# A decoder block on one core: the norm factor's broadcast moved, q and k turned in other lumps, q, k, v weights at another address, and the second norm's sum taken mid chunk

## Chip, cores and metric

The kernel runs on one core of a Trainium2 chip. The metric is the device time of one execution in microseconds: 377.47 us, the median of three runs (377.06 to 378.2). Lower is better.

## What is computed

One decoder layer over x (1, 256, 1024) in float32, cut to what matters:

```python
h = rms_norm(x, attn_norm_g)
qa, ka, va, qb, kb, vb, f_logit, g_logit = split(h @ w_in)     # six of 512 columns, 8, 2 x 1024
qa, ka = partial_rope(rms_norm(heads(qa))), partial_rope(rms_norm(heads(ka)))
o_a = causal softmax(qa ka^T / 8) va      # MoBA: with 256 tokens there is one block, so plain causal
qb, kb = rms_norm(heads(qb)), rms_norm(heads(kb))
c = cumsum(log_sigmoid(f_logit + b_forget))
o_b = causal softmax(qb kb^T / 8 + c[t] - c[s]) vb             # forgetting attention (FoX)
merged = sigmoid(g0 + b0) * (o_a @ w_branch_moba) + sigmoid(g1 + b1) * (o_b @ w_branch_fox)
x = x + merged @ w_out
u, g = split(rms_norm(x, ffn_norm_g) @ w_ffn_up)               # 2 x 2816 columns
x = x + (silu(causal_conv3(g) + b) * u) @ w_ffn_down
```

Eight heads of 64 in each branch.

## The kernel before

Everything is float32 at nearly full precision: each operand of a large product is split into a high part (fp32r, written by ScalarE, the whi or xh tiles) and the rest (by VectorE, wlo or xl), and each product is three matmuls, hi x hi, hi x lo and lo x hi. The weights come in 61 chunks of 128 x 2048 floats (1 MB), loaded by DMAs on SyncE's queue into one of three raw buffers. `load` splits a chunk in two halves of 1024 columns, each into one of six whi and six wlo tiles. `use(c, h)` hands out a half and has splits issued up to five halves ahead, so that ScalarE and VectorE work ahead of TensorE until the six buffers are full.

x is kept transposed (features on the partitions), as xh and xl times the norm's gain; the norm's factor rs per token is multiplied in after the products. The order of TensorE's instructions is that of the program text, by hand; the order on the other engines is a planner's, with dependencies, so it may change when the text is moved. PSUM has eight banks of 512 floats; all tiles there come from one pool of eight, and `banks()` takes two.

- `project(m, pt, h)`: one half of a q, k or v product (m = 0 to 2 the MoBA branch's q, k, v, 3 to 5 the FoX branch's), tokens on the partitions. 24 matmuls at line 217: 128 columns of xh or xl are loaded into the array and 512 columns of whi or wlo stream.
- `twin(kind, c, dst, mh, ml)`: a chunk of 2 x 128 output features, features on the partitions. 48 matmuls at lines 425 to 427: 128 columns of the weights are loaded and 256 tokens of mh or ml stream. The gates and the FFN's up product use it. Lines 512 to 514, 538 to 540 and 599 to 601 are the same form for the branch, out and down products.
- `norm1` (line 195): the sum of squares over partitions for rs; `rsqrt_mean` (lines 182 to 187) is VectorE, ScalarE's Ln and Exp, and three steps on VectorE.
- `rs_row` (413, 414): four matmuls with the identity broadcast rs to all partitions as rsB, which the gates read at line 432.
- `forget_a` to `forget_d` and `forget_bias`: the forget gate. `forget_a` (279, 283) multiplies by the eight gate columns wfg; `forget_b` (292 to 312) gives lf; `forget_c` (318 to 321) is the cumulative sum; `forget_d` (326 to 332) turns it, writes it to memory and reads it back on all partitions into one of the three raw buffers; `forget_bias` (339, 341) makes the bias from it.
- `finish_qk` (229 to 245): the heads' norms and rope; `turn_qk` (261, 266, 268): 16 transposes of 64 x 64, and copies by ScalarE and VectorE into qT or kT.
- `scores` (355) and `softmax` (367 to 375) for pairs of heads, `turn` (385, 388) turns the probabilities into pT, `values` (399, 403, 404) multiplies by V into oh and ol, `finish_v` (221) writes V.

The text that orders the first stage:

```python
    norm1(); rs_row(); forget_a()
    qn = finish_qk(pq, 0, 0)
    project(1, pk, 1)
    kn = finish_qk(pk, 0, 1)
    project(2, pv, 0); forget_b(); turn_qk(qn, 0, 0)
    project(2, pv, 1); turn_qk(kn, 0, 1); finish_v(pv, 0)
    project(3, pq, 0); forget_c(); scores(0, (0, 1))
    project(3, pq, 1); qn = finish_qk(pq, 1, 0); forget_d(); scores(0, (2, 3))
    project(4, pk, 0); turn(0, 0); turn(0, 1)
    project(4, pk, 1); kn = finish_qk(pk, 1, 1); turn(0, 2); turn(0, 3); turn_qk(qn, 1, 0)
    project(5, pv, 0); forget_bias(); values(0)
    project(5, pv, 1); turn_qk(kn, 1, 1); finish_v(pv, 1); gate(0)
```

The out product (line 540) is followed, for each pair of feature blocks, by the new x (543), its split into hh and hl (546, 547; these lie in the oh and ol buffers), its squares (549), and their running sum sqs on GpSimd (551 to 554). The FFN runs 22 chunks of `up`, two at a time, and after each pair but the first the `down` product of the pair before. In `up(0)` the sum of squares over partitions (565) and rs2 by `rsqrt_mean` follow the chunk's 48 matmuls. Behind them each `up` multiplies by rs2 (568), does the convolution (572 to 574), Silu (575), and splits the result (580, 581) into a tile in qT, kT or aT, which `down` streams.

Addresses: a tile's gaps at the head of the pool place the whi and wlo tiles at 32 mod 256 bytes; behind them a gap of 96 bytes and 16 bytes inside the tile place xh, xl, oh, ol and the later activations. All tiles between are multiples of 256 bytes long.

Of the kernel before, what the change touches and what calls it, by code (L numbers as in the profile page):

```python
# [9 lines left out]
F32R = mybir.dt.float32r  # L10
BF16 = mybir.dt.bfloat16
AF = mybir.ActivationFunctionType
# [5 lines left out]
P = 128  # L18
S = 256
NT = 2  # L20
D = 1024
KT = D // P
# [8 lines left out]
RB, HB, AHEAD = 3, 6, 5  # L31
# [10 lines left out]
def decoder_block(ctx, tc, a, out):  # L42
    nc = tc.nc
# [6 lines left out]
    def T(shape, tag, bufs=1, dt=F32):  # L50
        return sb.tile(shape, dt, tag=tag, bufs=bufs, name=tag)
# [11 lines left out]

    gap("gap0", GAPS[0])
    for tag in ("whi", "wlo"):
        T([P, 1024], tag, HB, F32R)
    gap("gap1", GAPS[1])
    for tag in ("xh", "xl", "oh", "ol"):
        T16(KT, tag)
# [19 lines left out]
    def load(upto):  # L89
        while state["next"] <= min(upto, 2 * len(chunks) - 1):  # L90
            i, h = divmod(state["next"], 2)
            c = chunks[i]
            n = 2 if i < 2 else 1
            if h == 0:
                w = 512 if i < 2 else 1024 if i == 2 else 2048
                src = a[c[0]]
                for j in c[1:]:
                    src = src[j]
                raw = state["raw"] = T([P, 2048], "raw", RB)
                for j in range(2048 // w):  # L100
                    if i < 2:
                        for k in XCUT.get(4 * i + j, ()):
                            load_x(k)
                    nc.sync.dma_start(raw[:, j * w:(j + 1) * w], src[:, j * w:(j + 1) * w])
            raw = state["raw"][:, h * 1024:(h + 1) * 1024]
            hi = T([P, 1024], "whi", HB, F32R)
            lo = T([P, 1024], "wlo", HB, F32R)
            w = 1024 // n
            for j in range(n):
                s = slice(j * w, (j + 1) * w)  # L110
                if i < 2:
                    split_x(2 * (2 * i + h) + j)
                nc.scalar.activation(hi[:, s], raw[:, s], AF.Copy)  # L113
                nc.vector.tensor_tensor(lo[:, s], raw[:, s], hi[:, s].bitcast(F32), op=ALU.subtract)  # L114
            split[c, h] = (hi, lo)
            state["next"] += 1
# [61 lines left out]
    def rsqrt_mean(dst, ss, n, shape, tag, bufs=2):  # L178

        w = T([P, 3] + shape, tag, bufs)  # L180
        v, y, t = w[:, 0], w[:, 1], w[:, 2]
        nc.vector.tensor_scalar(v, ss, 1.0 / n, EPS, op0=ALU.mult, op1=ALU.add)
        nc.scalar.activation(t, v, AF.Ln)
        nc.scalar.activation(y, t, AF.Exp, scale=-0.5)
        nc.vector.scalar_tensor_tensor(t, v, -0.5, y, op0=ALU.mult, op1=ALU.mult)
        nc.vector.tensor_tensor(t, t, y, op=ALU.mult)
        nc.vector.scalar_tensor_tensor(dst, t, 1.5, y, op0=ALU.add, op1=ALU.mult)

    rs = T([P, NT], "rs")
    rope = []  # L190
# [18 lines left out]
    def project(m, pt, h):  # L209
        for hh in range(2):  # L210
            wh, wl = use(("qkv", m, h), hh)
            for k2 in range(2):
                k = 4 * h + 2 * hh + k2
                rh, rl = wh[:, k2 * 512:(k2 + 1) * 512], wl[:, k2 * 512:(k2 + 1) * 512]
                for i, (lhs, rhs) in enumerate(((xh, rh), (xh, rl), (xl, rh))):
                    for t in range(NT):
                        nc.tensor.matmul(pt[t], lhs[:, k, t * P:(t + 1) * P], rhs, start=(k == 0 and i == 0), stop=(k == KT - 1 and i == 2))  # L217
# [70 lines left out]
    def forget_b():  # L288
        fs = fg["fs"]
        ft = bank()  # L290
        for t in range(NT):
            nc.tensor.matmul(ft[:, t * NH:(t + 1) * NH], fs[:, t * P:(t + 1) * P], sel, start=True, stop=True)
        z = T([P, NT, NH], "z")
        for t in range(NT):
            nc.vector.scalar_tensor_tensor(z[:, t], ft[:, t * NH:(t + 1) * NH], rs[:, t:t + 1], col(C_BF, NH), op0=ALU.mult, op1=ALU.add)

        az = T([P, NT, NH], "az")
        nc.scalar.activation(az, z, AF.Abs)
        e = T([P, NT, NH], "ez")
        nc.scalar.activation(e, az, AF.Exp, scale=-1.0)  # L300
        u = T([P, NT, NH], "uz")
        nc.vector.tensor_scalar_add(u, e, 1.0)
        l = T([P, NT, NH], "lz")
        nc.scalar.activation(l, u, AF.Ln)
        d = T([P, NT, NH], "dz")
        nc.vector.scalar_tensor_tensor(d, u, -1.0, e, op0=ALU.add, op1=ALU.subtract)
        r = T([P, NT, NH], "rz")
        nc.vector.reciprocal(r, u)
        nc.vector.tensor_tensor(d, d, r, op=ALU.mult)
        nc.vector.tensor_tensor(l, l, d, op=ALU.subtract)  # L310
        lf = T([P, NT, NH], "lf")
        nc.vector.scalar_tensor_tensor(lf, z, 0.0, l, op0=ALU.min, op1=ALU.subtract)
        fg["lf"] = lf
# [96 lines left out]
    def rs_row():  # L410
        rp = bank()
        for t in range(NT):
            nc.tensor.matmul(rp[:, t * P:(t + 1) * P], rs[:, t:t + 1].to_broadcast([P, P]), ident, start=True, stop=True)
        nc.vector.tensor_copy(rsB, rp[:, 0:S])

    def twin(kind, c, dst, mh, ml):

        for h in range(2):
            wh, wl = use((kind, c), h)
            for i in range(2):  # L420
                o = dst[:, i * S:(i + 1) * S]
                for k4 in range(4):
                    k = 4 * h + k4
                    w = slice(k4 * 256 + i * P, k4 * 256 + (i + 1) * P)
                    nc.tensor.matmul(o, wh[:, w], mh[:, k], start=(k == 0 and i == 0), stop=False)  # L425
                    nc.tensor.matmul(o, wh[:, w], ml[:, k], start=False, stop=False)  # L426
                    nc.tensor.matmul(o, wl[:, w], mh[:, k], start=False, stop=(k == KT - 1 and i == 1))  # L427

    def gate(c):
        gp = bank()  # L430
# [3 lines left out]
    def gate_sigmoid(c):  # L434
        for br in range(2):
            i = nc.scalar.activation(gates[:, c, br], gates[:, c, br], AF.Sigmoid, bias=col(C_BG + br * KT + c))
            after(i, last_exp[0])

    def after(i, j):
        tc.add_manual_dep(i.ins, j.ins.name, mybir.DependencyInfo(mybir.DependencyClass.NoSync, mybir.DependencyReason.DATA), reason="order")  # L440
# [6 lines left out]
    project(0, pq, 1)  # L447
    project(1, pk, 0)
    norm1()
    rs_row()  # L450
    forget_a()
    qn = finish_qk(pq, 0, 0)
    project(1, pk, 1)
    kn = finish_qk(pk, 0, 1)
    project(2, pv, 0)
    forget_b()
    turn_qk(qn, 0, 0)
    project(2, pv, 1)
    turn_qk(kn, 0, 1)
    finish_v(pv, 0)  # L460
    pq, pk, pv = banks(), banks(), banks()
    project(3, pq, 0)
    forget_c()
    scores(0, (0, 1))
    project(3, pq, 1)
    qn = finish_qk(pq, 1, 0)
    forget_d()
    scores(0, (2, 3))
    project(4, pk, 0)
    turn(0, 0)  # L470
    turn(0, 1)
    project(4, pk, 1)
    kn = finish_qk(pk, 1, 1)
    turn(0, 2)
    turn(0, 3)
    turn_qk(qn, 1, 0)
    project(5, pv, 0)
    forget_bias()
    values(0)
    project(5, pv, 1)  # L480
    turn_qk(kn, 1, 1)
    finish_v(pv, 1)
    gate(0)
# [11 lines left out]
    values(1)  # L495
    gate(6)
    gate(7)
    for c in range(KT):
        gate_sigmoid(c)


    mh = T16(KT, "xh")
# [57 lines left out]

    def up(f):
        up_ = bank()
        twin("wu", f, up_, hh, hl)
        if f == 0:
            nc.tensor.matmul(sp[:, 0:S], ones, sqs, start=True, stop=True)
            rsqrt_mean(rs2, sp[:, 0:S], D, [S], "pT", 4)
        ev = T([P, 2, S], "sq", 2)
        nc.vector.tensor_tensor(ev, up_.rearrange("p (b t) -> p b t", b=2), rs2[:, None, :].to_broadcast([P, 2, S]), op=ALU.mult)  # L568
        u, g = ev[:, 0], ev[:, 1]
        w = T([P, 3, S], "s", 4)  # L570
        cv, sl, av = w[:, 0], w[:, 1], w[:, 2]
        nc.scalar.activation(cv, g, AF.Identity, scale=col(C_CW + 2 * NF + f), bias=col(C_CB + f))
        nc.vector.scalar_tensor_tensor(cv[:, 1:], g[:, 0:S - 1], col(C_CW + NF + f), cv[:, 1:], op0=ALU.mult, op1=ALU.add)
        nc.vector.scalar_tensor_tensor(cv[:, 2:], g[:, 0:S - 2], col(C_CW + f), cv[:, 2:], op0=ALU.mult, op1=ALU.add)
        nc.scalar.activation(sl, cv, AF.Silu)
        nc.vector.tensor_tensor(av, u, sl, op=ALU.mult)
        if f % 2 == 0:
            acts[f // 2] = T16(4, ("qT", "kT", "aT")[f // 2 % 3])
        ah, al = acts[f // 2][:, f % 2], acts[f // 2][:, 2 + f % 2]
        nc.scalar.activation(ah, av, AF.Copy)  # L580
        nc.vector.tensor_tensor(al, av, ah.bitcast(F32), op=ALU.subtract)
# [24 lines left out]
                nc.sync.dma_start(out[:, ds[0]:ds[0] + n], y)  # L606

    for j in range(NF // 2):
        up(2 * j)
        up(2 * j + 1)  # L610
        if j > 0:
            down(j - 1)
    down(NF // 2 - 1)
# [66 lines left out]
```

## Time and profile before

| what | value |
|---|---|
| median of three runs | 377.47 us (377.06 to 378.2) |
| profiled execution | 377.7 us, span 375.9 us |
| granted TensorE clock | 1.00 |
| HBM read, written | 66.61 MB, 1.06 MB (180 GB/s over the span) |
| a 1 MB weight DMA, issue to landing | 4.8 us (median) |
| first split of a weight chunk's half: ScalarE, VectorE | 1058 ns, 1236 ns (128 x 1024) |

The span is the program from its first to its last instruction; the time of an execution is some 2 us more. In a timeline row stand start and duration in us, engine, line, operation, output and inputs, the number of instructions merged into the row, and in brackets how long the engine was idle before and what released it. The ends of matmuls are modelled, so their durations overlap; the distance between starts is what counts. PE is TensorE's matmuls, PEld its weight loads, DVE VectorE, ACT ScalarE, POOL GpSimd, SP SyncE.

### The profile page before, as it was taken

Reading aid. Unit: us, or ns where it says so; the run is one execution under the profiler, and the core shown is the slowest. Engines: PE = TensorE matmul, PEld = TensorE weight load, DVE = VectorE, ACT = ScalarE, POOL = GpSimd, SP = SyncE. Lnnn points to the kernel's source line nnn. Section 1 sums busy time; section 2 is a strip of 40 time slices with the busy share of each in tenths; the row PEclk is TensorE's granted clock in tenths of the full one; section 3 lists DMA queues with packets and bytes.
Section 4 is the critical chain, followed back from the end, with each engine's and each line's share of the span. In section 5 each row is a group of like instructions: output and inputs, shape, how many; then the busy total and the mean of one; then the engine's idle time right before and its main releaser. Section 6 shows DMA issues by size and latency. Waiting matters only on the chain.

```text
span 375.9 us, 7223 instructions
## 1 busy us (share of the span) xinstructions
PE 365.5 (97%) x2975; PEld 339.7 (90%) x2975; DVE 277.5 (74%) x486; ACT 214.4 (57%) x357; POOL 14.1 (4%) x18
## 2 busy tenths in 40 slices
PE   8979999999999999999999999999999999999995
PEld 3667877777999999999989999999999999999995
DVE  3879969997697455886787978677686867778653
ACT  4838557773579745445678755464555555455520
POOL 0320000000000000000070000000000000000000
PEclk9999999999999999999999999999999999999999
DMA  7995433648343643655554654565556455545003
GB/s 202 348 362 183 194 114 112 223 136 315 112 139 139 215 183 113 226 181 172 209 193 144 223 192 161 210 225 183 164 214 211 160 198 218 201 150 211 1 2 112
DMA packets 12002, 68.13 MB, mean 181 GB/s; under 512 B 1593, under 2 KB 2241, under 8 KB 4417
## 3 DMA queue, kind: packets, MB, share of 16 engines
q1 hardware_dynamic: 11664, 66.61, 49.9%
q10 hardware_dynamic: 304, 1.06, 0.8%
q8 instruction: 23, 0.38, 0.4%
q14 instruction: 11, 0.08, 0.1%
HBM read 66.61 MB, written 1.06 MB: 180 GB/s over the span
## 4 chain that ended last, share of the span: by engine, by line
PE 79%; DVE 9%; DMA 5%; ACT 3%; issue 1%; SPq 1%; POOLq 0%; POOL 0%; ACTq 0%; DVEq 0%
PE bank L425 14%; PE bank L426 14%; PE bank L427 14%; PE bank L217 8%; PE bank L599 5%; PE bank L600 5%; PE bank L601 5%; DMA raw<-in_qkv 4%; DVE wlo L114 3%; PE bank L512 2%; PE bank L514 2%; PE bank L513 2%; DMA raw<-in_wg 2%; PE bank L399 1%; PE bank L538 1%; PE bank L539 1%
## 5 line engine op out<-in xcount | busy, mean ns | idle before, releaser
L114 DVE TENSOR_TENSOR wlo<-raw,whi 128x1024 fp32r<-128x1024 f32 (+1 forms) x126 | 152.2, 1212 | 58.8 <-ACT whi L113 57.4
L113 ACT ACTIVATE whi<-raw 128x1024 fp32r<-128x1024 f32 (+1 forms) x126 | 129.3, 1030 | 98.2 <-PE bank L426 50.9
L426 PE MATMUL bank<-ol,whi 128*128 128x256 f32 x352 | 97.0, 276 | 0.2 <-DVE ol L547 0.2
L425 PE MATMUL bank<-oh,whi 128*128 128x256 f32 x352 | 97.0, 276 | 0.0
L427 PE MATMUL bank<-oh,wlo 128*128 128x256 f32 x352 | 96.9, 275 | 0.0
L426 PEld LDWEIGHTS bank<-ol,whi 128*128 128x128 f32 x352 | 66.1, 188 | 0.4 <-DVE ol L547 0.3
L425 PEld LDWEIGHTS bank<-oh,whi 128*128 128x128 f32 x352 | 66.1, 188 | 0.0
L427 PEld LDWEIGHTS bank<-oh,wlo 128*128 128x128 f32 x352 | 66.1, 188 | 0.0
L425 PE MATMUL bank<-xh,whi 128*128 128x256 f32 x128 | 35.9, 281 | 0.0
L426 PE MATMUL bank<-xl,whi 128*128 128x256 f32 x128 | 35.3, 276 | 0.0
L427 PE MATMUL bank<-xh,wlo 128*128 128x256 f32 x128 | 35.3, 276 | 0.0
L217 PE MATMUL bank<-whi,xh 128*128 128x512 f32 x96 | 31.8, 412 | 1.4 <-ACT pT L388 0.8
L217 PE MATMUL bank<-wlo,xh 128*128 128x512 f32 x96 | 31.0, 404 | 1.1 <-DVE wlo L114 1.1
L217 PE MATMUL bank<-whi,xl 128*128 128x512 f32 x96 | 30.2, 395 | 0.0
L425 PEld LDWEIGHTS bank<-xh,whi 128*128 128x128 f32 x128 | 24.0, 188 | 1.0 <-issue 0.5
L217 PEld LDWEIGHTS bank<-whi,xh 128*128 128x128 f32 x96 | 17.5, 190 | 8.1 <-ACT whi L113 2.0
L217 PEld LDWEIGHTS bank<-wlo,xh 128*128 128x128 f32 x96 | 17.8, 190 | 7.1 <-DVE wlo L114 3.2
L426 PEld LDWEIGHTS bank<-xl,whi 128*128 128x128 f32 x128 | 24.0, 188 | 0.0
L427 PEld LDWEIGHTS bank<-xh,wlo 128*128 128x128 f32 x128 | 24.0, 188 | 0.0
L217 PEld LDWEIGHTS bank<-whi,xl 128*128 128x128 f32 x96 | 18.1, 189 | 4.5
L568 DVE TENSOR_TENSOR sq<-bank,rs 128x512 f32<-128x512 f32 x22 | 15.1, 691 | 6.5 <-PE bank L427 6.5
L512 PE MATMUL bank<-oh,whi 128*128 128x256 f32 x64 | 17.6, 275 | 0.0
(163 smaller groups left out, 695.2 us busy)
## 6 DMA issues: line engine op xcount, KB each, us to landing
raw<-in_wu SPq DMA_DIRECT2D x22, 1024.0 KB, 4.8
raw<-in_wd SPq DMA_DIRECT2D x11, 1024.0 KB, 4.8
raw<-in_qkv SPq DMA_DIRECT2D x9, 1024.0 KB, 4.8
raw<-in_wg SPq DMA_DIRECT2D x8, 1024.0 KB, 4.9
raw<-in_wb SPq DMA_DIRECT2D x4, 1024.0 KB, 4.8
raw<-in_wo SPq DMA_DIRECT2D x4, 1024.0 KB, 4.8
raw<-in_qkv SPq DMA_DIRECT2D x8, 256.0 KB, 6.3
raw<-in_qkv SPq DMA_DIRECT2D x2, 512.0 KB, 7.1
```

The lines of the kernel that those rows point to most:

```text
L113: nc.scalar.activation(hi[:, s], raw[:, s], AF.Copy)
L114: nc.vector.tensor_tensor(lo[:, s], raw[:, s], hi[:, s].bitcast(F32), op=ALU.subtract)
L217: nc.tensor.matmul(pt[t], lhs[:, k, t * P:(t + 1) * P], rhs, start=(k == 0 and i == 0), stop=(k == KT - 1 and i == 2))
L425: nc.tensor.matmul(o, wh[:, w], mh[:, k], start=(k == 0 and i == 0), stop=False)
L426: nc.tensor.matmul(o, wh[:, w], ml[:, k], start=False, stop=False)
L427: nc.tensor.matmul(o, wl[:, w], mh[:, k], start=False, stop=(k == KT - 1 and i == 1))
L512: nc.tensor.matmul(o, wh[:, w], oh[:, 4 * br + k], start=(k == 0), stop=False)
L513: nc.tensor.matmul(o, wh[:, w], ol[:, 4 * br + k], start=False, stop=False)
L568: nc.vector.tensor_tensor(ev, up_.rearrange("p (b t) -> p b t", b=2), rs2[:, None, :].to_broadcast([P, 2, S]), op=ALU.mult)
L599: nc.tensor.matmul(o, wh[:, w], ah, start=(p == 0 and h == 0 and c == 0), stop=False)
L600: nc.tensor.matmul(o, wh[:, w], al, start=False, stop=False)
L601: nc.tensor.matmul(o, wl[:, w], ah, start=False, stop=(last and h == 1 and d == ds[-1]))
```

## The change

- `rs_row` moves from behind `norm1` to ahead of `forget_b`, which itself moves behind the whole of project(2).
- The turned q and k, scores, turns and values are put between other projections, as the diff shows.
- The whi and wlo tiles grow by 64 columns; in the q, k and v chunks the 1024 columns in use start at column 44, which is 208 mod 256 bytes, in all others at column 0 as before.
- In the first up chunk, the second half's outer loop runs over k. The sum over partitions and rs2 (now `norm2`) move into the middle of the second chunk, and the rest of chunk 0 (now `finish_up`) behind the second chunk's matmuls. The later chunks keep their order.
- ScalarE's table of Ln and Exp is loaded behind the sigmoids, and that of Silu behind the Exp of the second norm, by instructions of their own.

```diff
-        T([P, 1024], tag, HB, F32R)
+        T([P, 1088], tag, HB, F32R)
...
-            hi = T([P, 1024], "whi", HB, F32R)
-            lo = T([P, 1024], "wlo", HB, F32R)
+            at = 44 if c[0] == "qkv" else 0
+            hi = T([P, 1088], "whi", HB, F32R)[:, at:at + 1024]
+            lo = T([P, 1088], "wlo", HB, F32R)[:, at:at + 1024]
...
-        nc.scalar.activation(t, v, AF.Ln)
-        nc.scalar.activation(y, t, AF.Exp, scale=-0.5)
+        i = nc.scalar.activation(t, v, AF.Ln), nc.scalar.activation(y, t, AF.Exp, scale=-0.5)
...
+        return i
...
-    def twin(kind, c, dst, mh, ml):
+    def twin(kind, c, dst, mh, ml, late=False, between=None):
 
         for h in range(2):
             wh, wl = use((kind, c), h)
-            for i in range(2):
+            turns = [(i, k4) for k4 in range(4) for i in range(2)] if late and h else [(i, k4) for i in range(2) for k4 in range(4)]
+            for i, k4 in turns:
...
+            if h == 0 and between:
+                between()
...
     norm1()
-    rs_row()
     forget_a()
     qn = finish_qk(pq, 0, 0)
     project(1, pk, 1)
     kn = finish_qk(pk, 0, 1)
     project(2, pv, 0)
+    project(2, pv, 1)
+    rs_row()
     forget_b()
     turn_qk(qn, 0, 0)
-    project(2, pv, 1)
-    turn_qk(kn, 0, 1)
     finish_v(pv, 0)
     pq, pk, pv = banks(), banks(), banks()
     project(3, pq, 0)
     forget_c()
-    scores(0, (0, 1))
+    turn_qk(kn, 0, 1)
     project(3, pq, 1)
     qn = finish_qk(pq, 1, 0)
     forget_d()
+    scores(0, (0, 1))
+    project(4, pk, 0)
     scores(0, (2, 3))
-    project(4, pk, 0)
+    project(4, pk, 1)
+    kn = finish_qk(pk, 1, 1)
     turn(0, 0)
     turn(0, 1)
-    project(4, pk, 1)
-    kn = finish_qk(pk, 1, 1)
+    project(5, pv, 0)
+    forget_bias()
     turn(0, 2)
     turn(0, 3)
+    project(5, pv, 1)
+    values(0)
     turn_qk(qn, 1, 0)
-    project(5, pv, 0)
-    forget_bias()
-    values(0)
-    project(5, pv, 1)
     turn_qk(kn, 1, 1)
     finish_v(pv, 1)
     gate(0)
...
-    for c in range(KT):
-        gate_sigmoid(c)
+    sig = [gate_sigmoid(c) for c in range(KT)]
+    tables = [nc.scalar.preload_act_table_set("natural_log_exp_and_others")]
+    for i in sig:
+        after(tables[0], i)
...
-        twin("wu", f, up_, hh, hl)
-        if f == 0:
-            nc.tensor.matmul(sp[:, 0:S], ones, sqs, start=True, stop=True)
-            rsqrt_mean(rs2, sp[:, 0:S], D, [S], "pT", 4)
+        twin("wu", f, up_, hh, hl, f == 0, norm2 if f == 1 else None)
+        return up_
+
+    def norm2():
+        nc.tensor.matmul(sp[:, 0:S], ones, sqs, start=True, stop=True)
+        i = rsqrt_mean(rs2, sp[:, 0:S], D, [S], "pT", 4)
+        after(i[0], tables[0])
+        tables.append(nc.scalar.preload_act_table_set("silu_and_others"))
+        after(tables[1], i[1])
+
+    def finish_up(f, up_):
...
-        nc.scalar.activation(sl, cv, AF.Silu)
+        i = nc.scalar.activation(sl, cv, AF.Silu)
+        if f < 2:
+            after(i, tables[1])
...
     for j in range(NF // 2):
-        up(2 * j)
-        up(2 * j + 1)
+        u = up(2 * j)
+        if j > 0:
+            finish_up(2 * j, u)
+        v = up(2 * j + 1)
+        if j == 0:
+            finish_up(0, u)
+        finish_up(2 * j + 1, v)
         if j > 0:
             down(j - 1)
```

`after(i, j)` only orders i behind j in ScalarE's queue.

More of the change, by code (lines that the diff above doesn't have):

```diff
@@ L414, in rs_row @@
         nc.vector.tensor_copy(rsB, rp[:, 0:S])
-    def twin(kind, c, dst, mh, ml):
+    def twin(kind, c, dst, mh, ml, late=False, between=None):
         for h in range(2):
             wh, wl = use((kind, c), h)
-            for i in range(2):
+            turns = [(i, k4) for k4 in range(4) for i in range(2)] if late and h else [(i, k4) for i in range(2) for k4 in range(4)]
+            for i, k4 in turns:
                 o = dst[:, i * S:(i + 1) * S]
[L422 to L427, printed above, removed]
+                k = 4 * h + k4
+                w = slice(k4 * 256 + i * P, k4 * 256 + (i + 1) * P)
+                nc.tensor.matmul(o, wh[:, w], mh[:, k], start=(k == 0 and i == 0), stop=False)
+                nc.tensor.matmul(o, wh[:, w], ml[:, k], start=False, stop=False)
+                nc.tensor.matmul(o, wl[:, w], mh[:, k], start=False, stop=(k == KT - 1 and i == 1))
+            if h == 0 and between:
+                between()
     def gate(c):
@@ L437, in gate_sigmoid @@
             after(i, last_exp[0])
+        return i
     def after(i, j):
```

## The prediction

> **What bounds the kernel now.** I read the page first, then the windows by stage, then the timeline of TensorE (PE) around each place where the order changes, then VectorE (DVE), ScalarE (ACT) and GpSimd (POOL) at the same places.
>
> From the page: the span, the engines' busy time, and the chain that ended last.
>
> ```profile
> span 375.9 us, 7223 instructions
> ...
> PE 365.5 (97%) x2975; PEld 339.7 (90%) x2975; DVE 277.5 (74%) x486; ACT 214.4 (57%) x357; POOL 14.1 (4%) x18
> ...
> PE 79%; DVE 9%; DMA 5%; ACT 3%; issue 1%; SPq 1%; POOLq 0%; POOL 0%; ACTq 0%; DVEq 0%
> ```
>
> From the windows (us, then busy time of PE, PEld, DVE, ACT, POOL, granted clock, DMA share, GB/s):
>
> ```profile
> 29.50:49.30 19.80, 18.87 (x112) 15.06 (x108) 19.40 (x45) 13.39 (x23) 0.00 (x0) 1.00 0.47 167
> ...
> 64.70:79.50 14.80, 14.00 (x115) 11.02 (x113) 13.97 (x43) 11.11 (x30) 0.00 (x0) 1.00 0.47 164
> ```
>
> PE works almost without a break, at a granted clock of 1.00, and the edits end with the first two FFN chunks (about 204 us); what follows is the same loop as before. So a microsecond that PE loses less up to there comes off the end, as long as the other engines keep up. DVE is full (19.40 of 19.80 us) exactly where the order changes: that is the danger.
>
> **Lumps and waits.** The code between two runs of projection matmuls I call a lump. Each wait that the change touches has its rows ahead of it, PE's first.
>
> ```profile
> 26.04 0.50 PE L195 MATMUL bank<-ones,bias 128*128 128x1 f32 x4
> 27.84 0.71 PE L413 MATMUL bank<-cst,rs 128*128 128x128 f32 x4 [1.31 <-DVE rs L187]
> 28.48 1.07 PE L283 MATMUL bank<-xT,wfg 128*32 128x256 f32 x16
> ```
>
> ```profile
> 27.07 0.22 DVE L279 TENSOR_TENSOR wfg<-wfr,g 128x64 f32<-128x64 f32 x1
> ...
> 27.63 0.16 DVE L187 SCALAR_TENSOR_TENSOR rs<-rsv 128x2 f32<-128x2 f32 x1
> ```
>
> *rs_row moved.* Its four matmuls wait for rs (27.79) and take 0.64 us (27.84 to 28.48); forget_a stands behind them. Without them forget_a waits for wfg alone, which ends at 27.29; with the 0.05 us that lie between rs and L413 it starts at 27.34 instead of 28.48, 1.14 us sooner. The 0.64 us are paid later, ahead of forget_b. Net -0.50. If the DVE queue puts wfg behind rs, forget_a starts at about 28.05 and the net is +0.21: those are the two ends. I take -0.50, since wfg stands ahead of rs in the row. The copy of the row (L414) moves with it; its reader, the first gate, starts at 94.59 (below), so it is covered.
>
> ```profile
> 47.12 0.63 PE L217 MATMUL bank<-whi,xl 128*128 128x512 f32 x2
> 48.68 0.71 PE L261 MATMUL bank<-cst,qn 64*128 64x64 f32 x16 [0.93 <-DVE qn L245]
> ```
>
> ```profile
> 93.39 0.63 PE L217 MATMUL bank<-whi,xl 128*128 128x512 f32 x2
> 93.95 0.71 PE L261 MATMUL bank<-cst,qn 64*128 64x64 f32 x16
> 94.59 0.38 PE L425 MATMUL bank<-xh,whi 128*128 128x256 f32 x1
> ```
>
> *Turned k behind the next projection.* The last matmul of the x2 row at 47.12 starts at 47.35; L261 starts 1.33 us later. Where nothing waits, the same step takes 0.33 (the second of 93.39 starts at 93.62, then 93.95). So 1.00 us is a wait for L245, which ends a long chain on a full DVE. Behind 24 more matmuls (5.6 us) nothing is left to wait for: -1.00, ends -1.00 and -0.5 if the chain is rescheduled later. Late next on this path is lf: forget_b moves from 40.8 to about 46 while forget_c stays behind the first projection of the fox q, and the steps from z to lf (L295 to L312) took 7.2 us.
>
> ```profile
> 43.45 0.22 DVE L295 SCALAR_TENSOR_TENSOR z<-bank,rs,sm 128x8 f32<-128x8 f32 x1
> ...
> 50.51 0.16 DVE L312 SCALAR_TENSOR_TENSOR lf<-z,lz 128x16 f32<-128x16 f32 x1
> ```
>
> At the same pace lf comes at about 54 against a forget_c at about 53: +0.8 at worst. I take 0, because the k chain that stretched those 7.2 us is then done before them.
>
> ```profile
> 77.99 0.66 PE L261 MATMUL bank<-cst,qn 64*128 64x64 f32 x16
> 79.46 0.88 PE L217 MATMUL bank<-whi,xh 128*128 128x512 f32 x2 [0.80 <-ACT pT L388]
> ```
>
> *Fewer lumps.* Before there are nine in the qkv stage (norm; turned q; turned k; scores; scores; turns; turns with fox q; values; fox k), after it eight: fox q and fox k join values. A lump of one turn_qk alone costs 93.62 to 94.59 less a matmul's 0.23, plus 0.1 at the restart, 0.84 us; inside another lump, as in the row of 77.99, only its transposes remain, 0.66 less some 0.16 by which the last one's modelled end overlaps the next matmul, 0.5. So -0.34.
>
> *The bank wait at 79.46.* From L261's start to the next projection is 1.47 us; in the row of 93.95 it is 0.64. The 0.83 us, and 0.07 more at the restart, wait for ACT to copy pT out of the banks of the turns, while k's two banks and the three lumps' six leave none for v. After the change only two turns (four banks) stand ahead of v's projection, so two are free: -0.90, ends -0.90 and 0. In return values, two turn_qk and v (two banks each, eight) now stand ahead of gate 0, which needs one. DVE freed the second bank of values at 90.90 (below), 2.75 us behind its projection's start at 88.15. The turns take about 1.2 us of that, so up to +1.1; ACT frees other banks sooner, and I take +0.3.
>
> ```profile
> 89.62 1.28 DVE L404 TENSOR_TENSOR ol<-bank,oh 128x512 fp32r<-128x512 f32 x2
> ```
>
> forget_d moves ahead of scores with its transposes, its copy and its two DMAs on ACT's queue; these hold one of the three raw buffers, so SP's next loads wait, and ACT with them:
>
> ```profile
> 76.81 1.06 ACT L113 ACTIVATE whi<-raw 128x1024 fp32r<-128x1024 f32 x1 [3.11 <-DMA raw<-in_wg]
> ```
>
> That split, done at 77.87, is of weights first used at 94.59: 16.7 us hide the 3.11, so 0; held 3 us longer it would still be 0. finish_v and forget_bias keep their places against the projections.
>
> **The second norm.** PE at the end of chunk 0, at the sum, and at the first down product; then what each waits for:
>
> ```profile
> 193.97 0.28 PE L425 MATMUL bank<-oh,whi 128*128 128x256 f32 x1
> 194.40 0.39 PE L426 MATMUL bank<-ol,whi 128*128 128x256 f32 x1 [0.15 <-DVE ol L547]
> 194.62 0.28 PE L427 MATMUL bank<-oh,wlo 128*128 128x256 f32 x1
> ```
>
> ```profile
> 196.44 0.28 PE L427 MATMUL bank<-oh,wlo 128*128 128x256 f32 x1
> 197.13 0.70 PE L565 MATMUL bank<-sqs,cst 128*128 128x256 f32 x2 [0.41 <-POOL sqs L554]
> ```
>
> ```profile
> 214.05 0.28 PE L599 MATMUL bank<-qT,whi 128*128 128x256 f32 x1
> ```
>
> ```profile
> 193.87 0.87 DVE L547 SCALAR_TENSOR_TENSOR ol<-xT,sm,oh 128x256 fp32r<-128x256 f32 x2
> ```
>
> ```profile
> 195.42 1.66 POOL L554 TENSOR_TENSOR sqs<-sqs,sq 128x256 f32<-128x256 f32 x1
> ```
>
> ```profile
> 211.43 0.75 DVE L581 TENSOR_TENSOR qT<-s,qT 128x256 fp32r<-128x256 f32 x2
> ```
>
> With the outer loop over k, the second half of chunk 0 reaches k=6 after 12 matmuls and k=7 after 18 (1.36 and 2.04 us behind its start at about 193.3), and ol's two pieces are there at about 194.34 and 194.74: the steps of 0.43 and 0.22 us become 0.11 each, -0.43. The sum over partitions, put into the middle of chunk 1, comes 2.8 us behind chunk 0, when POOL (197.08) has long ended: its wait of 0.41 goes, its two matmuls stay, -0.41. The late finish of chunk 0 costs nothing while the first down product has its input: it started at 214.05, and qT was whole at 212.18, so 1.87 us of cover. The sum moves about 2 us later, and PE comes to the down product 0.8 us sooner: 2.8 us against that cover. Two table loads go out of the chain and a third goes ahead of the Silu:
>
> ```profile
> 197.72 1.28 ACT L183 ACT_TABLE_LOAD   x1
> ...
> 199.45 1.28 ACT L184 ACT_TABLE_LOAD   x1
> ...
> 207.27 1.28 ACT L575 ACT_TABLE_LOAD   x1 [0.23 <-DVE s L574]
> ```
>
> That is 2.56 us less to rs2 and 1.28 less at the Silu, 3.84 in all, which pays for the missing 0.9; without it PE would wait 0.9 us. So the loads themselves are worth 0. The first preload, 1.28 us of ACT behind the last sigmoid, is hidden by the weights that are split ahead there; at worst +1.28.
>
> **The address of the weights.** From the code: the old address is 208-176 = 32 mod 256, and xh lies at 32+96+16 = 144 (tiles are multiples of 256 bytes). In project the weights stream and xh is loaded; in twin it is the other way. PE at both, and at a restart of twin:
>
> ```profile
> 50.36 0.63 PE L217 MATMUL bank<-whi,xl 128*128 128x512 f32 x2
> ...
> 51.76 0.63 PE L217 MATMUL bank<-whi,xl 128*128 128x512 f32 x2
> ```
>
> ```profile
> 213.37 0.28 PE L425 MATMUL bank<-oh,whi 128*128 128x256 f32 x1
> ...
> 213.71 0.28 PE L425 MATMUL bank<-oh,whi 128*128 128x256 f32 x1
> ```
>
> ```profile
> 95.05 0.28 PE L425 MATMUL bank<-xh,whi 128*128 128x256 f32 x1
> ...
> 95.41 0.28 PE L425 MATMUL bank<-xh,whi 128*128 128x256 f32 x1
> ```
>
> Six matmuls of 512 columns start in 1.40 us, 233 ns each; three of 256 in 0.34, 113 ns, and 120 ns for some ten behind a restart. Two of 256 thus stream the same 512 columns in 227 ns, with a second start paid: a matmul of project loses 6.7 ns that one of twin does not. No run here shows the new address. (The twelve tiles grow by 256 bytes each, so all other addresses stay the same mod 256: 0.) The nearest row is twin's, so I take 227 ns. Ends: twice that gain (220 ns) and twin behind a restart (240 ns). Of the 288 matmuls, those behind the last wait for a first load count, 22 in this row of the chain of waits and nine half projections of 24:
>
> ```profile
> 20.80 5.40 PE bank L217 x22
> ```
>
> 238 x 6.7 ns = -1.6 us, ends -3.2 and +1.6.
>
> Of this a page of the Trainium skill says something else. "SBUF — State Buffer", Who interferes with whom, gives PE a read port for the moving operand and an independent one for weight loads, and says that PE never waits on anyone; by that the address is worth 0 and the gain is 1.6 us smaller. No row here tests it, since each stream has one address mod 256. "TensorE: Matmul & The Clock Gate", Back-to-back issue gap, lists 518 cycles for 512 columns, 216 ns at 2.4 GHz; the trace's 233 does not agree, and if the new address reached the page's figure, the part would be worth an estimated -4.1 us.
>
> **The sum.** -0.50 -1.00 -0.34 -0.90 +0.30 -0.43 -0.41 -1.6 = -4.9 us. The profiled execution took 377.7 us for a span of 375.9, 0.2 above the median of 377.47; both lose 4.9: span 371.0, median **372.6**.
>
> **The rivals.** *The address does nothing.* For it: L425 to L427 read xh, xl and oh, which lie 8448 bytes apart, at one 113 ns. Against it: the 6.7 ns. Then 372.6+1.6 = 374.2. It is the Trainium skill's rule above, and nothing in the trace refutes it. *The address gives double*: 372.6-1.6 = 371.0. *The waits come back*: DVE is the bound from 29.5 to 49.3 us and 64.7 to 79.5, so PE catches up with the splits of the weights or with the banks, and the 2.7 us of lumps are lost: 375.3. For it the 19.40 of 19.80 us; against it that the splits run ahead of their use. *Slower*: the new address makes stream and weight load collide. Behind the wait at 194.40 the next matmul starts 0.22 us later instead of 0.11: its weight load had no matmul to hide behind. At 0.11 us a matmul that is 26 us over 238; a quarter of it, 27 ns, gives 372.6+1.6+6.4 = 380.6. It decides from 3.3 us / 238 = 14 ns upward, 247 ns a matmul. Nothing in the trace speaks for so much, nothing excludes it.
>
> **How the numbers follow.** Forecast 0.42, address nothing 0.22, address double 0.17, waits come back 0.11, slower 0.08. A measurement of this kernel tells about 0.3% (1.1 us) from no change. All cases but the last are faster by more; of the waits case about half falls within it if the address adds its upper end too, and so does a small part of the last: faster 0.85, same 0.08, slower 0.07. The range takes in the address from 220 ns (371.0, with 0.8 us for waits that go better) to waits that come back: 370.2 to 375.8.
>
> **What would show it.** L217 starting every 227 ns; PE without a wait before turned k, before the fox v's first projection and at L565; four table loads instead of five, and none between Ln and Exp. A pitch of 233 refutes the address step; new idle time in front of L318, of gate 0's first L425 or of the first L599 shows the waits that I priced at 0, 0.3 and 0. The prediction is wrong above all if the pitch goes up, or if the DVE order of L279, L235 or L312 changes.

## The result, and the profile after

The kernel after takes **373.06 us** (median of four, 372.57 to 373.25) beside 377.31 for the kernel before on the same chip: a ratio of 0.9881, 95% interval 0.9862 to 0.9900, or -4.5 us (-3.8 to -5.2). The forecast was 372.6 in a range of 370.2 to 375.8. A second timing, on another chip, gave 372.43 beside 377.69, 0.9864 (0.9838 to 0.9891). The forecast change of -4.9 us lies inside both intervals; the first median is 0.46 us above the forecast, the second 0.17 below it.

The page of the kernel after: the span, the busy times, the chain that ended last.

```profile
span 371.5 us, 7223 instructions
...
PE 363.0 (98%) x2975; PEld 339.0 (91%) x2975; DVE 277.1 (75%) x486; ACT 213.5 (57%) x356; POOL 14.1 (4%) x18
...
PE 92%; DMA 4%; DVE 1%; SPq 1%; ACT 0%; issue 0%; DVEq 0%
```

DVE's share of the chain fell from 9% to 1% and ACT's from 3% to 0: PE now hardly waits for either. Where the time went is read by cutting both executions at the same places in PE's work: the norm's first matmul, the first gate, the first branch product, the first up product, the first down product, the end. Columns as in the prediction. First the kernel before:

```profile
26.04:94.59 68.55, 65.51 (x430) 50.89 (x428) 59.71 (x152) 43.55 (x91) 0.00 (x0) 1.00 0.51 188
94.59:147.05 52.46, 52.46 (x500) 50.19 (x497) 34.98 (x78) 35.58 (x75) 0.00 (x0) 1.00 0.44 152
147.05:190.57 43.52, 43.52 (x386) 43.52 (x385) 34.20 (x49) 24.44 (x35) 2.98 (x3) 1.00 0.55 192
190.57:214.05 23.48, 22.91 (x196) 22.47 (x195) 19.41 (x30) 17.82 (x25) 4.67 (x5) 1.00 0.51 176
214.05:375.91 161.86, 157.92 (x1394) 157.72 (x1392) 112.38 (x156) 78.26 (x111) 0.00 (x0) 1.00 0.47 167
```

and the kernel after:

```profile
26.57:91.42 64.85, 63.78 (x429) 50.95 (x427) 58.87 (x151) 44.71 (x92) 0.00 (x0) 1.00 0.55 196
91.42:143.86 52.44, 52.44 (x501) 50.17 (x497) 35.15 (x80) 34.44 (x74) 0.00 (x0) 1.00 0.44 156
143.86:187.38 43.52, 43.52 (x387) 43.52 (x385) 34.22 (x49) 25.72 (x36) 2.99 (x3) 1.00 0.54 192
187.38:209.61 22.23, 22.23 (x197) 22.18 (x196) 19.55 (x30) 15.53 (x23) 4.68 (x5) 1.00 0.48 180
209.61:371.46 161.85, 157.92 (x1394) 157.72 (x1392) 112.44 (x156) 78.28 (x111) 0.00 (x0) 1.00 0.48 168
```

Two stretches changed: from the norm to the first gate -3.70 us, the first two up chunks -1.25, together -4.95. The other three are the same to 0.02 us. What lies ahead of the norm, where PE waits for loads, took 26.57 instead of 26.04 us in this execution; in the second one profiled of the same kernel it took 25.76, with 64.84 and 22.23 us behind it and a span of 370.7. Over all executions profiled here the norm starts between 25.04 and 26.57 us, and every stretch behind it that an edit does not touch repeats to 0.1 us or better. So the stretches of a single trace settle an edit behind the norm to about 0.1 us, where the times need many runs to settle it to 1 us.

The places named in the prediction, on PE, in the kernel after. The norm's lump, the lump of forget_b with rs_row, the lump of forget_c with the turned k, the lump of values with both turned FoX products:

```profile
26.57 0.50 PE L196 MATMUL bank<-ones,bias 128*128 128x1 f32 x4
27.88 1.07 PE L284 MATMUL bank<-xT,wfg 128*32 128x256 f32 x16 [0.80 <-DVE wfg L280]
28.88 0.50 PE L218 MATMUL bank<-whi,xh 128*128 128x512 f32 x1
...
45.34 0.60 PE L414 MATMUL bank<-cst,rs 128*128 128x128 f32 x4
45.78 0.51 PE L293 MATMUL bank<-cst,pT 128*128 128x8 f32 x4
46.22 0.71 PE L262 MATMUL bank<-cst,qn 64*128 64x64 f32 x16
46.87 0.50 PE L218 MATMUL bank<-whi,xh 128*128 128x512 f32 x1
...
52.86 0.39 PE L319 MATMUL bank<-lf,cst 128*128 128x8 f32 x2 [0.27 <-DVE lf L313]
...
53.63 0.71 PE L262 MATMUL bank<-cst,qn 64*128 64x64 f32 x16
54.27 0.73 PE L218 MATMUL bank<-whi,xh 128*128 128x512 f32 x2
...
87.52 2.82 PE L400 MATMUL bank<-pT,V 128*64 128x256 f32 x32
90.27 1.22 PE L262 MATMUL bank<-cst,qn 64*128 64x64 f32 x32
91.42 0.38 PE L426 MATMUL bank<-xh,whi 128*128 128x256 f32 x1
```

The wait for rs (1.31) is gone and one for wfg (0.80) stands in its place; the wait for the turned k's input (0.93) is gone and one for lf has come; the gate at 91.42 waits for no bank. From the last projection start ahead of a lump to the first behind it, the lumps measure:

| lumps | before | after | change | forecast |
|---|---|---|---|---|
| norm; forget_b with the turned q (rs_row goes from one to the other) | 3.67 + 1.33 | 2.54 + 1.75 | -0.71 | -0.50 |
| turned k, forget_c, forget_d, scores | 1.97 + 2.40 + 2.05 | 2.06 + 2.05 + 1.83 | -0.48 | -1.00 |
| turns | 1.22 | 1.20 | -0.02 | 0 |
| turns, turned FoX q and k, values | 2.59 + 3.08 + 0.97 | 1.21 + 4.22 | -1.21 | -0.94 |
| sum | 19.28 | 16.86 | -2.42 | -2.44 |

The rest of the -3.70, -1.28 us, is the projections. The distance from one matmul's start to the next, their pitch, is now 227 ns in the steady part instead of 233: six steps lie between these two starts, 1.36 us apart.

```profile
50.17 0.61 PE L218 MATMUL bank<-wlo,xh 128*128 128x512 f32 x2
...
51.53 0.61 PE L218 MATMUL bank<-wlo,xh 128*128 128x512 f32 x2
```

### The profile page after: what moved, and what is told of

Same layout as the page of the kernel before. It is cut to its first block, busy times and chain, and to the rows that moved or that the text cites. A ratio compares the mean times of both kernels' runs of the same rounds, so it can differ in the third digit from the quotient of the medians.

```text
span 371.5 us, 7223 instructions
## 1 busy us (share of the span) xinstructions
PE 363.0 (98%) x2975; PEld 339.0 (91%) x2975; DVE 277.1 (75%) x486; ACT 213.5 (57%) x356; POOL 14.1 (4%) x18
## 4 chain that ended last, share of the span: by engine, by line
PE 92%; DMA 4%; DVE 1%; SPq 1%; ACT 0%; issue 0%; DVEq 0%
PE bank L426 15%; PE bank L428 15%; PE bank L427 15%; PE bank L218 14%; PE bank L616 5%; PE bank L614 5%; PE bank L615 5%; DMA raw<-in_qkv 4%; PE bank L545 2%; PE bank L519 2%; PE bank L546 2%; PE bank L544 2%; PE bank L520 2%; PE bank L518 2%; PE bank L356 2%; PE bank L400 1%
## 5 line engine op out<-in xcount | busy, mean ns | idle before, releaser
L426 PE MATMUL bank<-oh,whi 128*128 128x256 f32 x352 | 97.0, 276 | 0.0
L371 ACT ACTIVATE s<-s,nm 128x128 f32<-128x128 f32 (+1 forms) x32 | 14.2, 443 | 7.1 <-DVE nm L368 7.1
```

The costliest lines, as they stand in the source:

```text
L371: last_exp[:] = [nc.scalar.activation(s[:, j, c], s[:, j, c], AF.Exp, scale=-1.0, bias=nm[:, j, i:i + 1], accum_out=l[:, j, i:i + 1])]
```

## The experiments

All were made from the kernel before or after, and ratios are to the kernel before on the same chip.

**The address alone** (e1, from the kernel before), and **the address undone** (e2, from the kernel after):

```diff
 e1: -        T([P, 1024], tag, HB, F32R)
     +        T([P, 1088], tag, HB, F32R)
     +            at = 44 if c[0] == "qkv" else 0   # columns at:at + 1024 of hi and lo, as in the change
 e2: -            at = 44 if c[0] == "qkv" else 0
     +            at = 0
```

> The kernel before with the address of the q, k, v weights alone. Theory (the parts are independent, the address is worth 6.7 ns for each matmul of project behind the first loads): matmuls of project start every 227 ns, 1.3 to 1.6 us less than before, 375.7 to 376.0. Rival (the stage of before is held by its waits, so a faster product only waits longer): same pitch of 227 ns, but under 0.5 us less than before.

> The changed kernel with the address of before (column 0) in the grown tiles. Theory: project back at 233 ns, 1.3 to 1.6 us more than the changed kernel, 374.4 to 374.7. Rival (VectorE's splits and banks set the pace of the new order): under 0.5 us more, with waits that get shorter. If growing the tiles did it and not the start column, the pitch stays at 227 ns.

The stretch from the norm to the first gate, e1, then e2:

```profile
25.62:92.61 66.99, 64.30 (x429) 51.05 (x427) 59.62 (x152) 43.52 (x91) 0.00 (x0) 1.00 0.52 193
```

```profile
25.62:91.72 66.10, 65.11 (x430) 50.82 (x428) 59.15 (x152) 44.71 (x92) 0.00 (x0) 1.00 0.53 195
```

Steady matmuls of project start every 227 ns in e1 and every 233 in e2, so it is the start column that counts and not the longer tiles, which e2 has too. The address takes 68.55 to 66.99, -1.56 us, in the old order, and its loss costs 66.10 - 64.85 = 1.25 us in the new one; the up stretch stays where its kernel had it. Counted by the starts of the matmuls, the steps inside the projections give 1.22 us of it in e1 and 1.28 in e2. The other 0.3 us of e1 are lumps: the one with the bank wait shrank from 2.59 to 1.98 us, those of the turned q and the turned k grew by 0.17 and 0.14. The times say less: e1 took 376.05 us, 0.9976 (0.9964 to 0.9989), that is -0.9 us (-0.4 to -1.4). This lies between the 1.3 to 1.6 of its theory and the 0.5 of its rival, and why it falls short of the trace is open; e2 took 373.93, 0.9921 (0.9904 to 0.9939).

**The order undone, the second norm undone, the tables undone** (e3, e4, e5, each from the kernel after): the text of the first stage as before; the sum and rs2 behind chunk 0 and its finish ahead of chunk 1, with the plain loop; no table loaded by hand.

```diff
 e3:  project(2, pv, 0) ... gate(0) in the order of the kernel before, rs_row() behind norm1()
 e4: -        twin("wu", f, up_, hh, hl, f == 0, norm2 if f == 1 else None)
     +        twin("wu", f, up_, hh, hl)
     +        if f == 0:
     +            norm2()
 e5: -    tables = [nc.scalar.preload_act_table_set("natural_log_exp_and_others")]
     -        tables.append(nc.scalar.preload_act_table_set("silu_and_others"))
```

> The changed kernel with the old order of the first stage, from the first project to the first gate. Theory: the lumps' 2.4 us come back (norm 1.1 less the 0.4 paid later, turned k 1.0, one lump 0.3, banks 0.9, less 0.4 for lf), 375.3 to 375.7. Rival (the address gave part of the stage's gain by shifting when things are ready, so the old order loses less under it): under 1.5 us more.

> The changed kernel with the second norm at its old place (behind chunk 0, old loop order, chunk 0 finished at once); the two table preloads stay. Theory: 1.25 us more than the changed kernel as the traces' starts of the first up chunk and the first down product say, 374.3; by my sum 0.84, 373.9. Rival (the gain came from the tables): under 0.3 us more.

> The changed kernel without the two preloads of ScalarE's tables, which are then loaded in front of Ln, Exp and Silu as before. Theory (the loads are off TensorE's path; without them the cover of the first down product is 1 us short at worst): 0 to 0.9 us more than the changed kernel, most likely 0. Rival (the preloads carry the gain of the second norm): 1 us more or above, with TensorE idle in front of the first down product.

The changed stretch of e3 (norm to first gate), of e4 (up) and of e5 (first down product to the end):

```profile
25.04:92.25 67.21, 64.26 (x429) 51.05 (x427) 59.70 (x152) 43.49 (x91) 0.00 (x0) 1.00 0.53 193
```

```profile
186.82:210.23 23.41, 22.84 (x196) 22.39 (x195) 20.38 (x31) 15.18 (x23) 4.65 (x5) 1.00 0.50 177
```

```profile
208.55:371.74 163.19, 158.33 (x1394) 157.93 (x1392) 114.40 (x160) 79.23 (x114) 0.00 (x0) 0.99 0.47 167
```

Against the kernel after these are +2.36, +1.18 and +1.34 us; their other stretches are the same to 0.02. With e2's 1.25 the three parts that were said to bring something give 4.79 of the 4.95. The times: e3 374.65, 0.9944 (0.9925 to 0.9963); e4 373.64, 0.9909 (0.9890 to 0.9927); e5 373.51, 0.9911 (0.9892 to 0.9930).

The expectation of e5, "most likely 0", was missed, and its rival came true. PE waits inside the first down product, for the tile that comes last of the chain through rs2 and Silu: the second matmul starts 1.28 us behind the first instead of 0.11, and the slower matmuls of the restart add the rest. PE first, then ACT's table loads, both of e5:

```profile
208.55 0.36 PE L607 MATMUL bank<-qT,whi 128*128 128x256 f32 x1
209.83 0.39 PE L608 MATMUL bank<-qT,whi 128*128 128x256 f32 x1 [0.92 <-DVE qT L589]
```

```profile
195.65 1.28 ACT L184 ACT_TABLE_LOAD   x1
...
197.38 1.28 ACT L184 ACT_TABLE_LOAD   x1
...
205.20 1.28 ACT L583 ACT_TABLE_LOAD   x1 [0.80 <-DVE s L582]
```

and the two loads of the kernel after, neither of which stands in that chain:

```profile
145.88 1.28 ACT L503 ACT_TABLE_LOAD   x1
...
197.53 1.28 ACT L576 ACT_TABLE_LOAD   x1
```

So the loads by hand are worth next to nothing in the old place of the norm (e4 has them: an up stretch of 23.41 us beside 23.48 in the kernel before) and 1.34 us in the new one. That is more than the 1.18 us that the later norm brings: without the loads it would have brought nothing.

**Which address, and whose** (e6, e7). The kernel after with the weights of every half chunk at another multiple of 16 bytes; in the second scan x and the activations lie 64 bytes further on.

```diff
-            at = 44 if c[0] == "qkv" else 0
+            at = 4 * ((2 * i + h) % 16)
 second scan also:
-GAPS = (160, 96)
+GAPS = (160, 160)
```

> The changed kernel with another start column for each half chunk of weights, 0, 4, ... 60 in turn (16 bytes apart), in all chunks: one trace gives the pitch of each address, streamed (project) and loaded (twin and its like). Theory A (what counts is where the stream stands against the weight load, mod 256 bytes): project has 227 ns or less at some addresses and 233 or more at others, and so has twin, whose 113 ns is not the same at all 16. Theory B (only the stream's own address counts): project varies, twin stays at 113 ns at all 16, since its stream does not move. Theory C (the gain needs something else than the address): no dependence.

> The scan once more with xh, xl and all later activations 64 bytes further on (208 mod 256 instead of 144). Theory A: the good and bad columns of project and of twin are the same set shifted by 64 bytes. Theory B: project's set stays where it was (its stream did not move); twin's pitch changes as a whole or not at all. Theory C: no dependence.

The twentieth of the 22 up chunks is, in each scan, a pair of halves of 24 matmuls of twin, weights at 0 and at 16 mod 256, activations at 144 in the first scan and 208 in the second. First scan, then second:

```profile
343.48:346.20 2.72, 2.72 (x26) 2.72 (x25) 2.23 (x3) 1.55 (x2) 0.00 (x0) 1.00 0.43 181
346.20:349.07 2.87, 2.87 (x26) 2.87 (x25) 2.13 (x4) 1.47 (x3) 0.00 (x0) 1.00 0.71 228
```

```profile
343.28:346.14 2.86, 2.86 (x26) 2.86 (x25) 2.33 (x4) 1.55 (x2) 0.00 (x0) 1.00 0.35 146
346.14:348.86 2.72, 2.72 (x26) 2.72 (x25) 2.00 (x3) 1.37 (x2) 0.00 (x0) 1.00 0.73 241
```

At 0 the half takes 2.72 us in one scan and 2.86 in the other; at 16 it is the other way about. Neither operand's own address decides, but where they stand to each other. Over all halves a matmul of twin starts every 113 ns with the weights at 0, 32 and 208 in the first scan, at 64, 96 and 16 in the second, and every 117 to 120 at each of the other thirteen. Weights less activations, mod 256, that is 112, 144 and 64 both times. At each of the sixteen differences the typical pitch of the two scans agrees to 0.3 ns. In project, where the weights stream, 227 ns stand at 208 in the first scan and at 16 in the second, 64 both times; most others give 229 to 234. Each address has only 12 or 24 matmuls there, some of them among the first loads, and 227 also came up at other differences (16 in the first scan, 240 in the second) that the other scan did not confirm, so a second good one is not excluded. The old address, a difference of 144, is good for twin and bad for project; the new one, 64, is good for both, and none beat it. The scans as wholes took 383.21 and 382.98 us, one run each, since most addresses are bad ones.

**The waits that were left** (e8 to e11). Four kernels on one chip: the kernel after again, and three that change one or two things.

> The kernel after the change, unaltered, as the mark for the other three kernels on this chip. If only the start varies from run to run, the time from the first norm matmul to the first gate is 64.85 us within 0.1, the part from there to the end the same as in the first profile within 0.1, and the time within 0.6 us of 373.1. If the stages behind the start also wander, one of these differs by more than 0.1.

```diff
 e9:  +    turn_qk(kn, 0, 1)
           forget_c()
      -    turn_qk(kn, 0, 1)
 e10: as e9, and forget_a's product wfg ahead of norm1():
      +    nc.vector.tensor_tensor(wfg[:, :, 0:NH], wfr, g1[:, :, None].to_broadcast([P, KT, NH]), op=ALU.mult)
           norm1()
           forget_a()
 e11:      norm1()
      +    rs_row()
           forget_a()
      ...
      -    rs_row()
           forget_b()
```

> Turned k's transposes stand ahead of the three matmuls of forget_c instead of behind them. Theory: in the kernel after, that lump waits for lf (0.42 us above the step without a wait) while the turned k's input is long there; with the transposes first (some 0.7 us) lf, which came 0.1 us behind the end of the projection, is there before forget_c, and the lump shrinks from 2.06 to about 1.64 us: the time from the norm to the first gate falls from 64.85 to about 64.4, the whole by 0.4. Rival: the lump is bound by DVE, which runs its queue in the same order whatever PE does, and forget_c still waits as long: 64.85, no change in time. Second rival: the three small matmuls ahead of a restart cost as much as the wait did: 64.85 too, but with no row that waits for lf.

> The swap of the kernel before this one, and the product that makes wfg put on DVE's queue ahead of the norm's first step, so that forget_a need not wait for it. Theory: in the kernel after, forget_a idles 0.80 us for wfg, which stands behind five small operations of the norm on DVE while DVE was idle for 1.78 us before them; with wfg made in that idle time forget_a starts right behind the norm's four matmuls, the lump falls from 2.54 to about 1.75 us, and the time from the norm to the first gate to about 63.6: 1.2 us below the kernel after, of which 0.4 is the swap's. Rival: the load of wf lands as late as the norm's sum, DVE then waits for it ahead of the norm's chain, and the lump stays at 2.5 or grows: 64.4 or more. Second rival: the lump shrinks, but the first projection behind it waits for weights that DVE and ACT split, and the gain is given back in the next 5 us: 64.4.

> The kernel after with the broadcast of the norm's factor back behind the norm, all else kept. By the two traces: the norm's lump grows by 1.13 us and the lump of forget_b shrinks by 0.42, so that the time from the norm to the first gate rises from 64.85 to 65.56, 0.7 us. By the prediction's sum: 0.50, 65.35. Rival: the order of DVE's queue decides (the copy of the row then stands ahead of wfg or of the first squares), and the difference is 0 or over 1.2.

e8 repeats the first profile's stretches to 0.03 us; its time, 372.43, is 0.67 us below the 373.1 of the other chip, just outside the 0.6 that was expected. From the norm to the first gate, e9, e10 and e11 in that order (e8: 64.84):

```profile
26.20:90.61 64.41, 63.60 (x430) 50.88 (x428) 58.95 (x151) 44.55 (x92) 0.00 (x0) 1.00 0.55 197
```

```profile
25.62:89.77 64.15, 63.59 (x430) 50.89 (x428) 58.88 (x150) 44.49 (x92) 0.00 (x0) 1.00 0.55 200
```

```profile
25.42:90.89 65.47, 63.95 (x429) 51.02 (x428) 59.22 (x151) 44.75 (x92) 0.00 (x0) 1.00 0.53 196
```

e9 gains 0.43 us, as the wait for lf was sized: PE turns k while lf is made. e11 loses 0.63, close to the 0.7 that the lumps gave and above the prediction's 0.50. e10 was a partial miss: its norm lump did shrink, from 2.54 to 1.66 us (25.39 to 27.05), but only 0.26 us of the 0.88 arrived. PE of e10 at forget_a, then at forget_c:

```profile
25.62 0.50 PE L196 MATMUL bank<-ones,bias 128*128 128x1 f32 x4
26.05 1.07 PE L282 MATMUL bank<-xT,wfg 128*32 128x256 f32 x16
...
50.67 0.71 PE L262 MATMUL bank<-cst,qn 64*128 64x64 f32 x16
51.95 0.36 PE L317 MATMUL bank<-lf,cst 128*128 128x8 f32 x2 [0.56 <-ACT whi L114]
```

The profile names a split on ACT, but that had long begun; lf itself, on DVE, is the last thing made ahead of it, at 51.63 for 0.17 us:

```profile
51.63 0.17 DVE L311 SCALAR_TENSOR_TENSOR lf<-z,lz 128x16 f32<-128x16 f32 x1
```

Counted from the norm's first matmul, PE reached forget_b 0.90 us sooner than in e9 (18.30 instead of 19.20 us), but DVE reached z at the same place in both (21.47 and 21.46), and lf was there 26.18 us behind the norm instead of 26.22. DVE's queue, not PE, sets when lf comes, so 0.61 of the 0.88 us went into the wait. The theory of e10 had no place for this; its rivals put the loss elsewhere. The times of the four are 372.43, 371.78, 371.75 and 372.72 us with spreads of 0.5 to 1.0: the same order, too coarse to split 0.3.

**The sum later** (e12). e10 with forget_c one projection later and forget_d behind the scores:

```diff
     turn_qk(kn, 0, 1)
-    forget_c()
     project(3, pq, 1)
+    forget_c()
     qn = finish_qk(pq, 1, 0)
-    forget_d()
     scores(0, (0, 1))
+    forget_d()
```

> The kernel with wfg early and turned k ahead of forget_c, changed once more: forget_c stands one projection later, ahead of the first scores, and forget_d behind them. In the kernel before this one PE reached forget_c 0.9 us sooner and idled 0.56 us there for lf, whose chain on DVE and ACT starts only when DVE reaches z; 0.6 of the 0.9 us were so given back. Theory: with 24 more matmuls (5.6 us) ahead of it forget_c waits for nothing, its 0.66 us of matmuls only change their lump, and the time from the norm to the first gate falls from 64.14 to about 63.55, the whole to about 371.2. Rival: the cumulative sum's copy, and with it the transposes of forget_d, get stuck behind the softmax on DVE's queue, and PE waits there or for a bank: 64.1 or more. Second rival: the wait only moves to the next place where DVE is late (the second projection's weights or the scores' input): 64.1.

```profile
25.49:89.10 63.61, 63.59 (x429) 50.95 (x427) 57.37 (x148) 43.15 (x91) 0.00 (x0) 1.00 0.50 188
```

PE is busy in all but 0.02 us of the stretch, and the time is **370.94 us** (370.49 to 371.64), 0.9835 (0.9818 to 0.9852): the best version here, 0.3 to 0.5% below the kernel after by the ratios (0.9864 and 0.9881), 1.24 us by the stretches of the traces.

## Why the prediction was right, and where it was not

The sum was -4.9 us on the profiled execution. The stretches give -4.95. Ahead of the norm, where PE waits for loads and the prediction counted only the pitch of 22 matmuls, the first profile of the kernel after lost 0.53 us again and the second gained 0.28, which is why its span of 370.7 lies below the forecast 371.0. The mechanisms that were named are the ones that acted: the rs row, the address, the second norm and the table loads are each shown by an edit that undoes them; the turned k, the bank wait and the fewer lumps only together (e3), and by their rows. That the sum came out to 0.1 us is luck in part: behind it stand errors of 0.2 to 0.5 us, of both signs, that cancel.

- **rs_row** (-0.50): the mechanism held. wfg did stand ahead of rs on DVE, as chosen, and forget_a waits for it. Its price was -0.71 by the lumps, -0.63 by e11: behind the projection the four matmuls took 0.44 us (45.34 to 45.78), not the 0.64 that they took behind the wait for rs.
- **Turned k** (-1.00): the wait did go, but "I take 0" for lf was the step that failed: 0.65 us lie between the last projection start and forget_c, against 0.23 without a wait, and e9 got 0.43 back by reordering alone; a last 0.1 us of the difference is not traced to a row. The stated bound of +0.8 held it; the reason given for zero, that the k chain on DVE is done by then, did not. forget_b's matmuls ended at 46.29, but DVE was in the k chain, and the copy of the rs row that moved here, from 45.83 on and came to z only at 48.04; from z to lf it then took 4.8 us instead of 7.2. DVE of the kernel after:

```profile
48.04 0.22 DVE L296 SCALAR_TENSOR_TENSOR z<-bank,rs,sm 128x8 f32<-128x8 f32 x1
...
52.63 0.17 DVE L313 SCALAR_TENSOR_TENSOR lf<-z,lz 128x16 f32<-128x16 f32 x1
```

- **Bank wait and gate 0** (-0.90, +0.30) and **one lump** (-0.34): together -1.21 instead of -0.94. The bank wait went whole; the +0.30 for a late bank at gate 0 did not come. The prediction watched the banks of values, and these were late: DVE freed the last at 92.24, behind the gate's start at 91.42. But ACT's copies of V had freed v's two banks by 88.67, 2.75 us ahead of the gate, and of the eight banks named in the prediction these are the only two that were free in time. The upper end of +1.1 does not follow from its own numbers, which give 2.75 - 1.2 = 1.55. ACT and DVE of the kernel after:

```profile
87.40 1.27 ACT L222 ACTIVATE V<-bank,rs 128x512 f32<-128x512 f32 x2 [0.16 <-PE bank L218]
```

```profile
90.96 1.28 DVE L405 TENSOR_TENSOR ol<-bank,oh 128x512 fp32r<-128x512 f32 x2
```

- **The second norm** (-0.43 and -0.41): the up stretch lost 1.25 us, e4 gives 1.18. Chunk 0 now runs at 113 ns a matmul from end to end instead of a mean of 125 (-0.54). The step into the sum fell from 0.69 us (196.44 to 197.13) to 0.11, where the prediction took off only the 0.41 that the row labelled as a wait for POOL; and the sum's two passes start 0.22 us apart instead of 0.32. PE of the kernel after:

```profile
195.43 0.28 PE L428 MATMUL bank<-oh,wlo 128*128 128x256 f32 x1
195.54 0.59 PE L573 MATMUL bank<-sqs,cst 128*128 128x256 f32 x2
195.79 0.47 PE L426 MATMUL bank<-oh,whi 128*128 128x256 f32 x1
```

- **Tables** (0, and 0.9 without them): e5 put PE's wait at 0.92 us and the whole at 1.34. The prediction had the link right, that they pay for the later norm. As it said, four table loads are left instead of five, and none stands between Ln and Exp.
- **The address** (-1.6): the pitch is 227 ns, as twin's rows had suggested. The size agrees less well than -1.56 (e1) makes it look: 216 of the 238 matmuls lie between the norm and the gate, 1.45 us by the prediction's price, and there the steps of the projections gave 1.22 to 1.28, since some 190 of them gained the 6.6 ns and those right behind a wait did not. That column 44 would be a good one was taken from twin's pitch and from no row on addresses; by the scans most other columns would have brought less, so this hit is in part luck. The row cited for the rival, one pitch for xh, xl and oh 8448 bytes apart, said nothing: 8448 is 33 times 256. The rival that the address does nothing falls. With it falls here, as a statement on time, the rule of the Trainium skill's "SBUF — State Buffer", Who interferes with whom, that PE's two read ports are independent and PE never waits: 233 against 227 ns, and 117 to 120 against 113, with nothing but the addresses changed. Nor did any address reach the 518 cycles, 216 ns at 2.4 GHz, that the Trainium skill's "TensorE: Matmul & The Clock Gate", Back-to-back issue gap, lists for 512 columns; the best was 227 ns. The other rivals (address twice as good, waits that come back everywhere, a collision) did not show; of the waits one, lf's, came back.

## What to carry to other kernels

Cut two traces at the same events on the bounding engine and compare the stretches: here they repeat to 0.1 us where the times scatter by 1. When work is moved so that a wait goes, ask for the next input that becomes the last one, and check it again after every further gain, as e10 and e12 show; work that needs nothing new belongs ahead of work that waits. And try the address of one matmul operand against the other's before taking a pitch for the engine's limit.

## What the hardware showed that was not expected

- The pitch of these float32 matmuls depends on the difference of their two operands' addresses mod 256 bytes: 113 ns at differences (weights less activations) of 64, 112 and 144, and 117 to 120 ns at the other thirteen multiples of 16, for 256 streamed columns (e6, e7); for 512, 227 ns at 64 and 229 to 234 at most others. The mechanism is not shown.
- A table load on ACT takes 1.28 us, and the next activation starts at once behind it (a load at 195.65 in e5, the activation at 196.94). The set loaded by hand serves Ln and Exp both, while without it each of the two loads a table of its own (195.65 and 197.38).
